# Gated DeltaNet heads in a fused trunk layer: alternating row groups, decays from running sums, no zero-state products

## The chip, the cores and the metric

The kernel runs on one core of a Trainium2 chip. The metric is the device time of one execution in microseconds (us). The profile is of one execution on the same core. The engines are called PE (TensorE), PEld (its weight loads), DVE (VectorE), ACT (ScalarE), POOL (GpSimd) and SP (SyncE, which issues all DMAs here).

## The reference

One layer over 2048 positions of width 1024: RMSNorm, one input projection, three mixers (differential attention, gated DeltaNet, RG-LRU), gates, an output projection with a residual, and a final RMSNorm. The change is in the gated DeltaNet, 4 heads of width 128, cut here to what matters. The reference works in chunks of 64 positions, the kernel in chunks of 128, which gives the same result.

```python
beta = jax.nn.sigmoid(b)
g = -jnp.exp(a_log) * jax.nn.softplus(a + dt_bias)
# in chunks:
g = jnp.cumsum(g, axis=-1)
decay = jnp.exp(jnp.where(tri, g[..., :, None] - g[..., None, :], -jnp.inf))
Lmat = jnp.where(strict, einsum('bhnid,bhnjd->bhnij', k_beta, k) * decay, 0.0)
T = triangular_solve(eye + Lmat, eye, lower=True, unit_diagonal=True)
u = T @ v_beta
w = T @ (k_beta * jnp.exp(g)[..., None])
a_intra = jnp.where(tri, einsum('bhnid,bhnjd->bhnij', q, k) * decay, 0.0)
def step(state, xs):                       # state starts at zero
    v_new = u_i - w_i @ state
    o = (q_i * jnp.exp(g_i)[..., None]) @ state + a_i @ v_new
    state = state * jnp.exp(g_last) + (k_i * jnp.exp(g_last - g_i)).T @ v_new
```

## The kernel before

The sequence is worked in two halves of 1024 positions, each half in two sub-blocks (`sb`) of 512, and these in chunks of 128, eight to a half (`NC_H`). The first stage, up to about 1165 us, is the projection with the DeltaNet and the LRU; the second is the attention with the output projection.

In the first stage a list of jobs, 40 to a half, is worked through in a written order. A job is one weight block; `unit` multiplies it with one sub-block of the normalized input: 24 fp32r matmuls of 128x512 (L298 to L300; every operand is split in a high and a low part). `unit` calls `pump` three times, and the loop over the jobs once after it. `pump` takes every background generator in `bgs` one step further, to its next `yield`; so `wait(4)` is about one unit. Jobs of DeltaNet heads (key, query, value, gate) stand between jobs of attention and LRU. With a head's first key unit `Gdn.start` puts its `main` on the list.

`gb_post` turns the columns b and a of a half into beta, the log decays `g` of all four heads, and by matmul with a triangle of ones (`tri_le`) their running sums in each chunk; `gam` is the exponential of these, `gl` that of the chunk's total. `ghi` and `glo` are g split in two.

`main` waits until the key and query sub-blocks of its head are projected, convolved (POOL's first tap in L359, DVE's three in L363), passed through a SiLU (L371, L375) and transposed for their norms by `key_t` (L449): `v.nt` is then 4. After that, for each sub-block, POOL multiplies `tri_le` by columns of `ghi` and of `glo` (L522, 8 products of 128x128), PE sums them with two fp32r matmuls against `tri_gt` (L528, L531), ACT takes the exponential (L535), and the result `dec` is the decay between any two positions of a chunk. The products of keys with keys and queries (L543) are multiplied by it (L549).

The inverse of the unit triangular matrices is made by blocks: 32x32 blocks by substitution on DVE (L590, L596), which are loaded into `pi` and transposed into `xi` (L613); then pairs of 32x32 blocks are joined to 64x64 by small fp32 matmuls (L626, a copy to `zs32`, L635), and these to 128x128 (L650, L658). The two pairs of a chunk lie on partitions 0 to 63 and 64 to 127; their matmuls contract over partitions 0 to 31 and 64 to 95 in L626, and over 32 to 63 and 96 to 127 in L635. All of the first pair's stand ahead of all of the second's. L639 makes the transposed joint block of the first pair once more by itself for `xi` (L643). Last, the chunks are walked in order with the state `st`: keys times state (L674), the solved values (L683), queries times state (L685), the state's new term (L692), the intra-chunk output (L693).

Tiles come from rings by tag and number of buffers (`tp`: 3 PSUM banks; `s16`: 16; `sd`: 1). Each engine's order is laid down by the framework when the kernel is built, by its own planned times of operands and buffers, not simply in the order of the text; only what is marked `keep_in_program_order` stays. Each engine then runs its instructions in that order and waits at the head of it. Other lines that the rows name: L117 fetches a weight block, L287 and L291 split it, L852 and L854 split the output weights, L775 to L777 are gates of the LRU, L317 to L319 the value projection.

## Time and profile before

| | |
|---|---|
| median of 3 runs | 1781.47 us (1778.9 to 1782.03) |
| the profiled execution | 1784.56 us |
| its span | 1782.8 us |
| mean granted clock of PE | 0.991 |
| PE, DVE, ACT, POOL busy | 97%, 73%, 55%, 20% |
| DMA, share of 16 engines | 49.5% |
| DMA moved | 257.45 MB |

Busy time is the time in which an engine has an instruction in work. Matmuls are pipelined, so that their times overlap: what one of them costs is the distance from its start to the next one's start. Durations and waits below are those of the profiled execution; its own time is its span and what lies around it.

### The profile page before, as it was taken

To read this page: it belongs to the slowest core of one execution; us is meant where nothing else is said; L and a number is where in the kernel's file an instruction comes from. 1 tells how busy PE (TensorE), PEld (TensorE's weight loads), DVE (VectorE), ACT (ScalarE), POOL (GpSimd) and SP (SyncE) were. 2 spreads that over 40 slices of the span, in tenths; PEclk is the share of its full clock that TensorE was granted. 3 is DMA by queue.
4 is the path that set the end of the run, shared out by engine and by line. 5 is a ranking of instruction groups with operands and counts; after the bars stand their busy time and mean duration, and the time that the engine had idled before them with its cause. 6 is when DMAs were issued, how large, how long until landed. Compare 5 with 4: busy or idle time off the path is not lost. (4 is left out here: it accounts for less than half of the span.)

```text
span 1782.8 us, 28375 instructions
## 1 busy us (share of the span) xinstructions
PE 1727.3 (97%) x9674; PEld 1440.2 (81%) x9674; DVE 1305.5 (73%) x3064; ACT 987.1 (55%) x2500; POOL 364.0 (20%) x591
## 2 busy tenths in 40 slices
PE   7999999999999899999999999989999999999998
PEld 6877778888888887887888888877888888887786
DVE  5576786776786656778687678658787877778896
ACT  6524524524535453452443443458878878878684
POOL 3222521400400212031040040011212213221011
PEclk9998999999999999999999999999999999999999
DMA  6146465133135432313313324597798797596442
GB/s 185 48 125 198 142 198 160 48 101 94 57 108 164 143 86 69 92 48 100 92 50 113 90 68 128 162 260 217 188 251 221 253 252 208 166 274 217 158 142 101
DMA packets 306901, 257.45 MB, mean 144 GB/s; under 512 B 66794, under 2 KB 242116, under 8 KB 306756
## 3 DMA queue, kind: packets, MB, share of 16 engines
q1 hardware_dynamic: 306756, 255.64, 49.5%
q8 instruction: 76, 1.25, 0.3%
q14 instruction: 69, 0.57, 0.1%
HBM read 171.69 MB, written 83.89 MB: 143 GB/s over the span
## 5 line engine op out<-in xcount | busy, mean ns | idle before, releaser
L298 PE MATMUL pj<-hp,wx 128*128 128x512 f32 x1120 | 465.6, 416 | 5.0 <-DVE s L375 2.9
L300 PE MATMUL pj<-hp,wx 128*128 128x512 f32 x1120 | 445.8, 398 | 0.0
L299 PE MATMUL pj<-hp,wx 128*128 128x512 f32 x1120 | 444.5, 397 | 0.0
L300 PEld LDWEIGHTS pj<-hp,wx 128*128 128x128 f32 x1120 | 211.4, 189 | 49.6
L298 PEld LDWEIGHTS pj<-hp,wx 128*128 128x128 f32 x1120 | 212.3, 190 | 48.3 <-DVE s L375 3.5
L299 PEld LDWEIGHTS pj<-hp,wx 128*128 128x128 f32 x1120 | 212.7, 190 | 41.6
L1030 DVE TENSOR_REDUCE nm<-s 128x1 f32<-128x512 f32 (+3 forms) x320 | 191.6, 604 | 27.5 <-PE s L1027 24.1
L1038 ACT ACTIVATE s<-s,nm 128x512 f32<-128x512 f32 (+3 forms) x272 | 170.6, 629 | 51.9 <-DVE nm L1030 50.7
L363 DVE SCALAR_TENSOR_TENSOR s<-raw,pcol,s 128x512 f32<-128x512 f32 x192 | 144.6, 753 | 36.3 <-POOL s L359 34.4
L1026 PE MATMUL s<-hp 128*128 128x512 f32 (+3 forms) x320 | 125.2, 392 | 6.2 <-ACT s L1038 3.1
L291 DVE TENSOR_TENSOR wx<-wx 128x1024 fp32r<-128x1024 f32 (+1 forms) x77 | 95.9, 1246 | 45.9 <-ACT wx L287 45.1
L287 ACT ACTIVATE wx<-wx 128x1024 fp32r<-128x1024 f32 (+1 forms) x76 | 80.5, 1059 | 80.5 <-PE pj L299 72.5
L1027 PE MATMUL s<-hp 128*128 128x512 f32 (+3 forms) x320 | 118.4, 370 | 0.0
L1101 PE MATMUL pt<-ident,s 128*128 128x128 f32 x544 | 86.4, 275 | 4.0 <-DVE s L1089 3.9
L354 POOL COPY halo<-raw 128x3 f32<-128x3 f32 x48 | 13.5, 281 | 374.0 <-ACT raw L352 364.9
L883 PE MATMUL pj<-g,wx 128*128 128x512 f32 x208 | 85.4, 411 | 0.0
L590 DVE TENSOR_TENSOR tt<-lt,tt 128x248 f32<-128x248 f32 (+30 forms) x248 | 80.4, 324 | 6.6
L596 DVE TENSOR_TENSOR tt<-tt 128x248 f32<-128x248 f32 (+30 forms) x248 | 79.2, 320 | 6.3
L1089 DVE SCALAR_TENSOR_TENSOR s<-s,cf,s 128x512 f32<-128x512 f32 (+2 forms) x112 | 75.1, 702 | 11.1 <-ACT s L1077 6.5
L885 PE MATMUL pj<-g,wx 128*128 128x512 f32 x208 | 82.3, 396 | 0.0
L884 PE MATMUL pj<-g,wx 128*128 128x512 f32 x208 | 82.0, 394 | 0.0
L317 PE MATMUL pj<-wx,hp 128*128 128x264 f32 (+1 forms) x256 | 77.1, 302 | 3.2 <-ACT hp L267 1.5
(341 smaller groups left out, 3966.5 us busy)
## 6 DMA issues: line engine op xcount, KB each, us to landing
wx<-in_w_in_dram SPq DMA_DIRECT2D x78, 512.0 KB, 4.1
wx<-y_sp SPq DMA_DIRECT2D x64, 512.0 KB, 5.5
hp<-k_sp SPq DMA_DIRECT2D x64, 256.0 KB, 6.3
wo_sp<-s SPq DMA_DIRECT2D x48, 256.0 KB, 2.5
v_sp<-s SPq DMA_DIRECT2D x64, 128.0 KB, 2.9
q_sp<-s SPq DMA_DIRECT2D x32, 256.0 KB, 3.6
k_sp<-s SPq DMA_DIRECT2D x32, 256.0 KB, 4.1
y_sp<-go SPq DMA_DIRECT2D x32, 256.0 KB, 2.1
```

The costliest lines, as they stand in the source:

```text
L291: pin(eng.tensor_tensor(wl, wr, wh.bitcast(F32), op=ALU.subtract))
L298: nc.tensor.matmul(ps, wh[:, kt, :], hb[kt][:, 0, :], start=(kt == 0), stop=False)
L299: nc.tensor.matmul(ps, wh[:, kt, :], hb[kt][:, 1, :], start=False, stop=False)
L300: nc.tensor.matmul(ps, wl[:, kt, :], hb[kt][:, 0, :], start=False, stop=(kt == KT - 1))
L363: nc.vector.scalar_tensor_tensor(y, raw[:, t : t + SB], pc(wcol(t)), y, op0=ALU.mult, op1=ALU.add)
L883: nc.tensor.matmul(ps, yh, wh, start=first, stop=False)
L885: nc.tensor.matmul(ps, yl, wh, start=False, stop=last)
L1026: nc.tensor.matmul(ps[:, :n], qq, kh[:, :n], start=True, stop=False)
L1027: nc.tensor.matmul(ps[:, :n], qq, kl[:, :n], start=False, stop=True)
L1030: nc.vector.tensor_reduce(nm[:, u, m, kb : kb + 1], ps[:, :n], axis=AX.X, op=ALU.max, negate=True)
L1038: nc.scalar.activation(ee[:, :n], ps[:, :n], AF.Exp, bias=nm[:, u, m, kb : kb + 1], accum_out=zp[:, u, m, kb : kb + 1],)
L1101: nc.tensor.transpose(pt[:, off + (u - us[0]) * P : off + (u - us[0] + 1) * P], e[(u, kt // 4)][:, (kt % 4) * P : (kt % 4 + 1) * P], ident,)
```

## The change

- The loops of L626 and L635 are turned round: chunk outside, pair inside, so that matmuls of the two row groups alternate in PE's order. A chunk's fp32 matmul is two instructions, so the alternation is by twos.
- L639 is dropped: the block for `xi` is a DVE transpose of the block that `pi` now holds.
- The decays no longer come from matmuls. `gb_post` makes one more matmul per half, the running sums of all heads and chunks as rows, copies them to SBUF and stores them in DRAM (`cs`). With a head's first key unit, two DMAs load the head's four rows for each sub-block, broadcast to all 128 partitions, into two buffers of `sd`. After `wait(4)` POOL subtracts in place each position's own sum (`cum`) and takes the minimum with zero (4 instructions of 128x128 for each sub-block, where 8 were), and ACT takes the exponential. `ghi`, `glo`, `tri_gt` and the `wait(3)` in front of the matmuls go.
- The first chunk of half 0 leaves out the two products with the zero state (L674, L685), and the last chunk of half 1 the state that nobody reads (L692, with its DVE operations). The four memsets of the state go.

```diff
--- before.py
+++ after.py
@@ -148,12 +148,6 @@
     nc.gpsimd.affine_select(
         tri_le, ones32, pattern=[[1, P]], compare_op=ALU.is_ge, fill=0.0, base=0, channel_multiplier=-1
     )
-    tri_gt = ctile([P, P], "tri_gt", F32R)
-    tri_gt32 = at([P, P], "s16", 16)
-    nc.gpsimd.affine_select(
-        tri_gt32, ones32, pattern=[[-1, P]], compare_op=ALU.is_gt, fill=0.0, base=0, channel_multiplier=1
-    )
-    nc.vector.tensor_copy(tri_gt, tri_gt32)
 
     pcol = ctile([P, N_COLS], "pcol")
     nps = psum.tile([P, SB], F32, name="pps", tag="tp", bufs=3)
@@ -172,8 +166,6 @@
     hlast = ctile([P, 4], "hlast")
     st2 = [at([P, 2, P], "st", 2) for _ in range(2)]
     st = [st2[h // 2][:, h % 2, :] for h in range(4)]
-    for h in range(4):
-        nc.gpsimd.memset(st[h], 0.0)
 
 
     def tp():
@@ -401,10 +393,6 @@
         g = at([P, 4, NC_H], "g", 2)
         nc.vector.scalar_tensor_tensor(g, xa, 0.0, ax, op0=ALU.max, op1=ALU.add)
         nc.vector.tensor_tensor(g, g, nea.unsqueeze(2).to_broadcast([P, 4, NC_H]), op=ALU.mult)
-        ghi = at([P, 4, NC_H], "ghi", 2, F32R)
-        nc.vector.tensor_copy(ghi, g)
-        glo = at([P, 4, NC_H], "glo", 2, F32R)
-        nc.vector.tensor_tensor(glo, g, ghi.bitcast(F32), op=ALU.subtract)
         yield
         yield
         yield
@@ -412,13 +400,21 @@
         gf = g.rearrange("p a b -> p (a b)")
         nc.tensor.matmul(pg[:, 0:32], tri_le, gf, start=True, stop=True)
         nc.tensor.matmul(pg[:, 32:64], ones, gf, start=True, stop=True)
+        nc.tensor.matmul(pg[0:32, 64 : 64 + P], gf, tri_le, start=True, stop=True)
         gam = at([P, 2, 4, NC_H], "gam", 2)
         nc.scalar.activation(
             gam, pg[:, 0:64].rearrange("p (a b c) -> p a b c", a=2, b=4), AF.Exp
         )
+
+        cum = at([P, 4, NC_H], "cum", 1)
+        nc.scalar.activation(cum, pg[:, 0:32].rearrange("p (b c) -> p b c", b=4), AF.Copy)
+        cr = at([32, P], "s16", 16)
+        nc.scalar.activation(cr, pg[0:32, 64 : 64 + P], AF.Copy)
+        cs = dram.tile([4 * NC_H, P], F32, name="cs", tag="cs", bufs=2)
+        nc.sync.dma_start(cs, cr)
         ngam = at([P, 4, NC_H], "ngam", 2)
         nc.vector.tensor_scalar_mul(ngam, gam[:, 0], -1.0)
-        r.beta, r.ghi, r.glo, r.gam, r.gl, r.ngam = beta, ghi, glo, gam[:, 0], gam[:, 1], ngam
+        r.beta, r.cum, r.cs, r.gam, r.gl, r.ngam = beta, cum, cs, gam[:, 0], gam[:, 1], ngam
         r.ready = True
 
 
@@ -488,7 +484,26 @@
 
         def main(v):
             h, gbs = v.h, v.gbs
-            while v.nt < 4 or not gbs.ready:
+            while not gbs.ready:
+                yield
+            decs = [at([P, 4, P], "sd", 2) for _ in range(2)]
+            for sb in range(2):
+                r0 = h * NC_H + sb * 4
+                nc.sync.dma_start(
+                    decs[sb].rearrange("p c e -> p (c e)"),
+                    gbs.cs[r0 : r0 + 4].rearrange("r e -> (r e)").unsqueeze(0).to_broadcast([P, SB]),
+                )
+            yield from wait(4)
+            for sb in range(2):
+                for c in range(4):
+                    ci = sb * 4 + c
+                    nc.gpsimd.tensor_scalar(
+                        decs[sb][:, c, :], decs[sb][:, c, :], gbs.cum[:, h, ci : ci + 1], 0.0,
+                        op0=ALU.subtract, op1=ALU.min,
+                    )
+                nc.scalar.activation(decs[sb], decs[sb], AF.Exp)
+                yield
+            while v.nt < 4:
                 yield
             ss = v.ss
             nc.vector.tensor_scalar_add(ss, ss, 4e-6)
@@ -514,25 +529,8 @@
                 kq = v.kq[sb]
                 la = at([P, 4, 2, P], "g5", 5)
                 las.append(la)
-                gmh = at([P, 4, P], "s16", 16, F32R)
-                gml = at([P, 4, P], "s16", 16, F32R)
-                for c in range(4):
-                    ci = sb * 4 + c
-                    for gm, gg in ((gmh, gbs.ghi), (gml, gbs.glo)):
-                        nc.gpsimd.tensor_scalar(
-                            gm[:, c, :], tri_le, gg.bitcast(F32)[:, h, ci : ci + 1], 0.0,
-                            op0=ALU.mult, op1=ALU.add,
-                        )
-                yield from wait(3)
-                pe = tp()
-                nc.tensor.matmul(
-                    pe, tri_gt, gmh.rearrange("p c e -> p (c e)"), start=True, stop=False
-                )
-                nc.tensor.matmul(
-                    pe, tri_gt, gml.rearrange("p c e -> p (c e)"), start=False, stop=True
-                )
-                dec = at([P, 4, P], "sd", 1)
-                nc.scalar.activation(dec, pe.rearrange("p (c e) -> p c e", c=4), AF.Exp)
+
+                dec = decs[sb]
                 nc.vector.tensor_tensor(
                     cd[:, sb * 4 : sb * 4 + 4], cc[:, sb * 4 : sb * 4 + 4], dec[:, :, P - 1],
                     op=ALU.mult,
@@ -621,8 +619,8 @@
             ]
             zs32 = at([P, NC_H, 32], "zs", 1)
             pz = tp().rearrange("p (c e) -> p c e", c=NC_H)
-            for a, b in pairs:
-                for c in range(NC_H):
+            for c in range(NC_H):
+                for a, b in pairs:
                     nc.tensor.matmul(
                         pz[b, c, 0:32], lt_ab(c, a, b), xi[a, c, a], start=True, stop=True
                     )
@@ -630,19 +628,15 @@
                 nc.vector.tensor_copy(zs32[b], pz[b, :, 0:32])
             yield
             pu = tp().rearrange("p (c e) -> p c e", c=NC_H)
-            for a, b in pairs:
-                for c in range(NC_H):
+            for c in range(NC_H):
+                for a, b in pairs:
                     nc.tensor.matmul(
                         pu[a, c, 0:32], zs32[b, c, :], pi[b, c, b], start=True, stop=True
                     )
-            for c in range(NC_H):
-                nc.tensor.matmul(
-                    pu[32:64, c, 0:32], pi[32:64, c, 32:64], zs32[32:64, c, :],
-                    start=True, stop=True,
-                )
-            nc.vector.tensor_scalar_mul(xi[32:64, :, 0:32], pu[32:64, :, 0:32], -1.0)
             for a, b in pairs:
                 nc.vector.tensor_scalar_mul(pi[a, :, b], pu[a, :, 0:32], -1.0)
+
+            nc.vector.transpose(xi[32:64, :, 0:32], pi[0:32, :, 32:64])
             yield
             lo, up = slice(0, 64), slice(64, 128)
             pz = tp().rearrange("p (c e) -> p c e", c=NC_H)
@@ -670,36 +664,51 @@
                 so = at([P, 4], "so", 2)
                 for c in range(4):
                     ci = sb * 4 + c
-                    pks = psum.tile([P, P], F32, name="ch", tag="ch", bufs=2)
-                    nc.tensor.matmul(pks, v.kq[sb][:, c, 0, :], S_, start=True, stop=True)
+
+                    none, final = v.hf == 0 and ci == 0, v.hf == 1 and ci == NC_H - 1
                     ct = at([P, 4, P], "ct", 2)
-                    br = ct[:, 0, :]
-                    nc.vector.scalar_tensor_tensor(
-                        br, pks, gbs.ngam[:, h, ci : ci + 1], v.vb[sb][:, c, :],
-                        op0=ALU.mult, op1=ALU.add,
-                    )
-                    yield
+                    br = v.vb[sb][:, c, :]
+                    if not none:
+                        pks = psum.tile([P, P], F32, name="ch", tag="ch", bufs=2)
+                        nc.tensor.matmul(pks, v.kq[sb][:, c, 0, :], S_, start=True, stop=True)
+                        br = ct[:, 0, :]
+                        nc.vector.scalar_tensor_tensor(
+                            br, pks, gbs.ngam[:, h, ci : ci + 1], v.vb[sb][:, c, :],
+                            op0=ALU.mult, op1=ALU.add,
+                        )
+                        yield
                     py = psum.tile([P, P], F32, name="ch", tag="ch", bufs=2)
                     nc.tensor.matmul(py, pi[:, ci, :], br, start=True, stop=True)
                     po = psum.tile([P, 2, P], F32, name="oq", tag="oq", bufs=1)
-                    nc.tensor.matmul(po[:, 0, :], v.kq[sb][:, c, 1, :], S_, start=True, stop=True)
-                    yd = ct[:, 1, :]
-                    nc.vector.tensor_scalar(yd, py, cd[:, ci : ci + 1], None, op0=ALU.mult)
+                    if not none:
+                        nc.tensor.matmul(
+                            po[:, 0, :], v.kq[sb][:, c, 1, :], S_, start=True, stop=True
+                        )
+                    if not final:
+                        yd = ct[:, 1, :]
+                        nc.vector.tensor_scalar(yd, py, cd[:, ci : ci + 1], None, op0=ALU.mult)
                     y = ct[:, 2, :]
                     nc.scalar.activation(y, py, AF.Copy)
                     yield
-                    pst = psum.tile([P, P], F32, name="ch", tag="ch", bufs=2)
-                    nc.tensor.matmul(pst, v.kp[sb][:, c, :], yd, start=True, stop=True)
+                    if not final:
+                        pst = psum.tile([P, P], F32, name="ch", tag="ch", bufs=2)
+                        nc.tensor.matmul(pst, v.kp[sb][:, c, :], yd, start=True, stop=True)
                     nc.tensor.matmul(po[:, 1, :], las[sb][:, c, 1, :], y, start=True, stop=True)
-                    nc.vector.scalar_tensor_tensor(
-                        S_, S_, gbs.gl[:, h, ci : ci + 1], pst, op0=ALU.mult, op1=ALU.add
-                    )
-                    ay = ct[:, 3, :]
-                    nc.scalar.activation(ay, po[:, 1, :], AF.Copy)
-                    nc.vector.scalar_tensor_tensor(
-                        os_[:, c, :], po[:, 0, :], gbs.gam[:, h, ci : ci + 1], ay,
-                        op0=ALU.mult, op1=ALU.add,
-                    )
+                    if none:
+                        nc.vector.tensor_copy(S_, pst)
+                    elif not final:
+                        nc.vector.scalar_tensor_tensor(
+                            S_, S_, gbs.gl[:, h, ci : ci + 1], pst, op0=ALU.mult, op1=ALU.add
+                        )
+                    if none:
+                        nc.scalar.activation(os_[:, c, :], po[:, 1, :], AF.Copy)
+                    else:
+                        ay = ct[:, 3, :]
+                        nc.scalar.activation(ay, po[:, 1, :], AF.Copy)
+                        nc.vector.scalar_tensor_tensor(
+                            os_[:, c, :], po[:, 0, :], gbs.gam[:, h, ci : ci + 1], ay,
+                            op0=ALU.mult, op1=ALU.add,
+                        )
                     jk = at([P, SB], "junk", 1, BF16)
                     nc.scalar.activation(
                         jk[:, :P], os_[:, c, :], AF.Square, accum_out=so[:, c : c + 1]
@@ -913,7 +922,7 @@
                     if last:
                         nw.append(load_wo(4 + e, 1, e) if dh == 0 else load_wo(e % 4, e // 4, e))
                     yield
-                pe = at([P, SB], "sd", 1)
+                pe = at([P, SB], "sd", 2)
                 nc.scalar.activation(pe, ps, AF.Copy)
                 nc.gpsimd.tensor_tensor(xx, pe, xx, op=ALU.add)
                 late.append(partial(nc.sync.dma_start, xo_sp[rows, cols], xx))
```

## Rows read from the trace of the kernel before

**Rows 1.** Page, part 1: busy us, share of the span, instructions of each engine.
```profile
PE 1727.3 (97%) x9674; PEld 1440.2 (81%) x9674; DVE 1305.5 (73%) x3064; ACT 987.1 (55%) x2500; POOL 364.0 (20%) x591
```

**Rows 2.** Windows by stage: stretch, us, busy us (instructions) by engine, PEclk, DMA.
```profile
60.00:230.00 170.00, 163.88 (x835) 131.29 (x834) 119.17 (x268) 75.93 (x187) 59.27 (x97) 0.97 0.44 135
...
820.00:1165.00 345.00, 344.50 (x1957) 284.55 (x1956) 251.10 (x600) 141.44 (x328) 52.75 (x104) 1.00 0.35 102
```

**Rows 3.** Waits of PE: line <- who released it: us, times, longest.
```profile
PE tp L635 <- POOL s L854: 2.1, 1, 2.1
...
PE tp L528 <- POOL s L522: 1.4, 3, 0.6
...
PE tp L543 <- DVE g L549: 0.9, 4, 0.2
```

**Rows 4.** Timeline of PE in the second head's inverse: start us, us, instruction.
```profile
284.87 1.09 PE L626 MATMUL tp<-xi,g 32*32 32x32 f32 x32
...
288.88 1.00 PE L635 MATMUL tp<-g,zs 32*32 32x32 f32 x29
289.69 0.21 PE L639 MATMUL tp<-zs,g 32*32 32x32 f32 x1
289.72 0.19 PE L635 MATMUL tp<-g,zs 32*32 32x32 f32 x1
...
289.81 0.57 PE L639 MATMUL tp<-zs,g 32*32 32x32 f32 x13
```

**Rows 5.** Timeline of PE at a decay product.
```profile
355.02 0.40 PE L528 MATMUL tp<-s,tri_gt 128*128 128x512 f32 x1
355.26 0.39 PE L531 MATMUL tp<-s,tri_gt 128*128 128x512 f32 x1
355.87 1.97 PE L543 MATMUL tp<-g 128*128 128x256 f32 x8 [0.22 <-DVE g L549]
```

**Rows 6.** Timeline of PE at a state product.
```profile
177.60 0.38 PE L674 MATMUL ch<-st,g 128*128 128x128 f32 x2
177.74 0.48 PE L298 MATMUL pj<-hp,wx 128*128 128x512 f32 x1
178.05 0.40 PE L299 MATMUL pj<-hp,wx 128*128 128x512 f32 x1
178.29 0.40 PE L300 MATMUL pj<-hp,wx 128*128 128x512 f32 x1
```

**Rows 7.** Groups by line: busy us, mean ns of one, idle before.
```profile
L522 POOL TENSOR_SCALAR s<-tri_le,glo 128x128 fp32r<-128x128 f32 x64 | 31.5, 492 | 0.0
L522 POOL TENSOR_SCALAR s<-tri_le,ghi 128x128 fp32r<-128x128 f32 x64 | 27.2, 426 | 0.4 <-issue 0.4
...
L613 DVE STREAM_TRANSPOSE xi<-g 32x256 f32<-32x256 f32 x24 | 10.4, 434 | 10.5 <-DMA g<-ts 10.0
```

**Rows 8.** DMA issues: KB each, median us to landing.
```profile
hp<-k_sp SPq DMA_DIRECT2D x64, 256.0 KB, 6.3
...
s<-in_w_out_dram SPq DMA_DIRECT2D x24, 256.0 KB, 3.6
```

**Rows 9.** Waits of SP's queue: us, times, longest.
```profile
SPq L117 <- DVE wx L291: 184.5, 32, 17.0
```

**Rows 10.** Timeline of a key sub-block of the first head.
```profile
77.78 0.69 DVE L375 SCALAR_TENSOR_TENSOR g<-s,s 128x512 f32<-128x512 f32 x1 [0.70 <-ACT s L371]
...
80.39 0.60 PE L449 MATMUL tp<-ident,g 128*128 128x128 f32 x4
```

**Rows 11.** Windows in the first head, behind the stall of L635.
```profile
161.50:170.50 9.00, 9.00 (x43) 6.81 (x42) 3.45 (x6) 0.60 (x1) 1.23 (x4) 0.50 0.82 193
```

**Rows 12.** Timeline of PE in that stretch.
```profile
162.08 0.63 PE L299 MATMUL pj<-hp,wx 128*128 128x512 f32 x1
162.50 0.63 PE L300 MATMUL pj<-hp,wx 128*128 128x512 f32 x1
```

**Rows 13.** Groups by line: the split of the output weights.
```profile
L852 ACT ACTIVATE s<-s 128x512 fp32r<-128x512 f32 x24 | 14.9, 622 | 6.2 <-DMA s<-in_w_out_dram 6.2
```

## The prediction, before the change was run

> **What bounds the kernel now.** I read the busy shares first. TensorE is busy for 97% of the span, DVE for 73%, ACT for 55% and POOL for 20% [rows 1]. A busy TensorE need not be a full one, so the table by stage comes next: in the last projection stretch it is busy for 344.5 of 345 us at full granted clock, and in the stretch with the first head for 163.9 of 170 us at 0.97 [rows 2]. There a unit of 24 fp32r matmuls follows the next, start to start 0.23 to 0.24 us [rows 6], which is the time the 512 columns take; the 0.40 us that the rows give as duration is a pipeline and not a cost. So in the first 1165 us, where every edited line runs, TensorE issues almost without a hole, and an instruction removed from its queue is worth its start-to-start distance. The waits of TensorE on the edited lines are short [rows 3]. DVE, ACT and POOL matter only where one of them is late for a TensorE instruction. I expect nothing in the attention stage, where the edits only give `sd` a second buffer.
>
> **Sum, part by part.** The profiled execution took 1784.56 us (span 1782.8, 1.8 around it), 0.17% above the median 1781.47 of the runs shown. I sum against the profiled time and then take the same off the median.
>
> *Alternating row groups and the dropped block.* An fp32 matmul is two instructions here. L626 is 2 pairs x 8 chunks x 2 = 32 of them per head. From first start to last start they take 1.09 - 0.19 = 0.90 us (the last end less the 0.19 us that one lasts, as the single rows show). L635 and L639 are 48 and take from 288.88 to 290.38 - 0.19, which is 1.31 us [rows 4]. Within one row group the step is (0.57 - 0.19)/12 = 0.032 us, from the thirteen L639. But where the last L635 (partitions 96 to 127) meet the first L639 (32 to 63), the two mix: L639 at 289.69, an L635 at 289.72 that lasts 0.19 as ever, and so on. Two row groups thus run beside each other, and what hinders that today is only the order: the second group's instructions stand 16 places behind, and begin when three of the first are left. In the new order pairs of instructions alternate, so the two groups should overlap throughout: 16 x 0.032 = 0.51 us plus a little for the later group, 0.53. Per head that saves 0.90 - 0.53 = 0.37 and 1.31 - 0.53 = 0.78 us (L639 gone with it), together 1.15, and 8 heads (4 heads x 2 halves) give **9.2 us**. The bounds are no overlap at all (32 x 0.032 = 1.02 us a block, so 1.31 + 0.90 - 2.04 = 0.17 a head, **1.4 us**) and a perfect one (0.48 a block, 1.25 a head, 10.0 us). I take a value near the upper end because the overlap is in the rows. The DVE transpose that now fills the block of `xi` costs 0.43 us [rows 7], where a scaling of the same 32x256 elements stood; it comes after the two scalings of `pi` rather than before them, about 0.9 us later (two more DVE operations of that size), while a yield puts six matmuls or 1.4 us in front of the next block.
>
> The Trainium skill, TensorEngine Tiling (Array Packing), section Restrictions and Gotchas, speaks against this part: different row tiles, it says, cannot access the same PSUM bank at the same time. Both pairs write one bank of `pz` or `pu`. By that rule the lower bound 1.4 us would hold in place of 9.2. The trace disagrees so far: the mixed L635 and L639 of rows 4 write one `pu` tile. The skill's TensorE: Matmul & The Clock Gate, Part 1 (on the gap of 56 ns), adds that start-to-start never falls under about 25 ns; an estimate from that page is 0.8 us a block and some 5 us of gain. The mixed rows, 0.01 to 0.03 apart, are under it for a few instructions only.
>
> *Decays.* L528 and L531 go: 16 pairs (8 heads x 2 sub-blocks), 0.24 us each [rows 5], so 32 x 0.235 = 7.5 us. Their waits go too: 1.4 us for POOL's products, and 0.9 us that L543 stood for a PSUM buffer of which L531's tile held one of three [rows 3]. Together **9.8 us**, with 7.5 as lower bound if those waits find another owner. POOL's 128 products at 0.43 to 0.49 us [rows 7] become 64 subtract-and-min of the same shape: some 29 us less on an engine at 20%. The Exp stays on ACT, reading SBUF. Sixteen broadcast loads of 256 KB are new on SP's queue, and two 16 KB stores; they add 4.2 MB. What that can cost is the third rival.
>
> *Zero state.* For the first chunk of each head in half 0, two fp32 matmuls go (4 heads x 2), and for the last chunk in half 1 one (4 heads): 12. One costs 0.22 us: L674 starts at 177.60 and L299 at 178.05, 0.45 us with one L298 of 0.23 in between [rows 6]. **2.6 us.** DVE work removed here is off the path.
>
> *Added.* The transposed running sum is one fp32 matmul per half, 2 x 0.22 = **0.4 us** lost. The copies of `cum` and `cr` are small ACT work in front of it.
>
> Sum: 9.2 + 9.8 + 2.6 - 0.4 = 21.2 us. 1784.56 - 21.2 = 1763.4 for a profiled execution; 1781.47 - 21.2 = 1760.3 for the median, and I say **1760.5**.
>
> **What could be late next.** Each engine runs an order that the framework lays down while building, from its own planned times, so edits can move neighbours. One bad spot of before shows the size: in the first head L635 stood 2.1 us, by the row for POOL's L854 [rows 3], and behind that the granted clock is 0.50 from 161.5 to 170.5 us [rows 11], which of the two levels is 1.2 GHz; the wide matmuls there start 0.42 us apart [rows 12] in place of 0.23. Nine us at that pace hold the work of 4.9, so 4.1 us were lost, with the stall 6.2. If this spot goes, that much comes back; if another like it arises, as much is lost. I take zero and keep both ends, 1754 and 1767.
>
> **Rivals.** (a) *The row groups do not overlap*, by bank or by issue: 21.2 - (9.2 - 1.4) = 13.4 us, so **1768**. Against it stand the mixed rows; for it, that they show only a few instructions. Chance 0.10, with a partial overlap, between 1761 and 1768, included. Both pages' rules above end in this rival.
> (b) *The neighbourhood is laid out better*: the stall and the half clock of the first head vanish, **1754**. The second head's L635, at 288.88 [rows 4], has no wait in its row. Chance 0.10.
> (c) *The broadcast comes late and holds POOL* (the other side). The new subtractions wait in POOL's order for a 256 KB load issued four yields earlier, 4 x 6 matmuls, 5.6 us. Such loads land in 3.6 to 6.3 us after issue [rows 8], and SP's own queue can stand up to 17 us before a weight load [rows 9]. Behind POOL's waiting instruction stand the key convolution's first tap (L359), then DVE's taps, the SiLU and TensorE's transposes of the key (L449). The slack is small: the SiLU result for one sub-block ended at 78.47 and its transposes began at 80.39, 1.9 us [rows 10]. A load that is d us late on POOL costs TensorE d - 1.9. With 16 of them, d = 1.9 + 21.2/16 = 3.2 us eats the whole gain, and 4 us each gives 1760.3 + 16 x 2.1 = **1794**. Against it: the 24 loads of output weights, also 256 KB and used six yields after issue, let ACT wait 6.2 us in all [rows 13]; four yields is only 2.8 us less, and the planner can put the tap first. Chance 0.07.
> (d) *Removed work turns into waits*: TensorE reaches the DVE results of the inverse sooner and stands there, so that nine tenths of the 21.2 us are given back, **1779** (no change). DVE has 27% free [rows 1], which speaks against it. Chance 0.05.
> The forecast itself has 0.68.
>
> **Range and chances.** 0.2% of 1781, 3.6 us, is about what a measurement of this kernel can tell from no change. The range takes in (a) and (b) and some late broadcasts (half the case (c), one us beyond the slack each, 1776): 1752 to 1775. Faster: forecast, (a), (b) 0.88. Same: 0.05. Slower: 0.07.
>
> **What would show it.** Right: 32 instructions per inverse block within 0.75 us (0.53 plus the tail), and no third block; TensorE with 180 instructions fewer (32 + 128 + 24 - 4); the new POOL subtractions without idle time for a DMA before them; the last projection stretch again full, and the attention stage as long as before. Wrong: blocks still 0.9 us or longer (a); POOL idle before the subtractions for the broadcast and L449 waiting for DVE (c); new waits of TensorE on DVE in the inverse (d). The prediction fails most easily by a stall with a clock fall behind it, in either direction, since one is a third of the whole gain.

## The result, and the profile after

The changed kernel takes 1795.04 us (median of 4 runs, 1793.55 to 1795.3) beside 1781.75 us for the kernel before (4 runs, 1778.9 to 1785.72): **1.0053 times as long, 95% interval 1.0037 to 1.0069**. The forecast was 1760.5 us, range 1752 to 1775, with 0.07 for slower: wrong in sign. The profiled execution took 1795.14 us, its span 1793.3 us at a mean granted clock of 0.989.

The work went as forecast. Part 1 of the page after has the 180 TensorE instructions fewer that were counted [rows 1]:

```profile
PE 1712.6 (96%) x9494; PEld 1421.5 (79%) x9494; DVE 1298.1 (72%) x3043; ACT 987.3 (55%) x2504; POOL 350.9 (20%) x522
```

The blocks of the inverse overlap. TensorE's timeline in the second head (the lines L624 and L633 are L626 and L635 of [rows 4]) shows one block of 32 in 0.69 - 0.19 = 0.50 us where 0.53 was said, and no third block:

```profile
275.08 0.69 PE L624 MATMUL tp<-xi,g 32*32 32x32 f32 x32
...
279.12 0.69 PE L633 MATMUL tp<-g,zs 32*32 32x32 f32 x32 [0.37 <-issue]
```

Eleven of the sixteen blocks take this time. The other five take 0.75 to 1.34 us, with projection matmuls or waits of 0.2 to 0.5 us between their first instructions and the rest.

The table by stage (columns as in [rows 2]) shows what did not go as forecast: the last projection stretch has holes. TensorE is busy for 347.8 of 355 us, where before 344.5 of 345, and in the stretch with the first head for 159.5 of 170, where before 163.9:

```profile
60.00:230.00 170.00, 159.53 (x811) 127.27 (x809) 117.98 (x266) 75.70 (x188) 54.01 (x85) 0.98 0.46 139
820.00:1175.00 355.00, 347.83 (x1934) 284.46 (x1934) 256.57 (x618) 146.93 (x339) 47.75 (x87) 1.00 0.36 104
```

The waits of TensorE after name the largest. In the changed kernel the projection of [rows 6] stands at L290 to L292, the value projection at L309, the key products at L541 and their scaling at L547; the wait of L541 is the 0.9 us of L543 in [rows 3], grown to 13.8:

```profile
PE tp L541 <- DVE g L547: 13.8, 7, 5.0
...
PE pj L309 <- DVE s L325: 4.7, 2, 3.4
...
PE tp L445 <- DVE g L367: 2.6, 2, 2.4
```

To see all holes at once I took from the records, for each line of TensorE, the median distance from one start to the next. The median times the count, summed over the lines, is "work"; what a distance has above its line's median, where that is over 0.3 us, is a stall. Beside them stands the time at the granted clock 0.50, the lower of the two levels (1.2 GHz); some 2 us of it lie behind the last instruction in every run.

| kernel | span | work | stalls | at clock 0.50 |
|---|---|---|---|---|
| before | 1782.8 | 1696.2 | 51.4 | 33.9 |
| after | 1793.3 | 1677.8 | 80.3 | 41.6 |

Work fell by 18.4 us; the prediction's removed and added instructions come to 21.2 - 2.3 of waits = 18.9. Stalls rose by 28.9 us, and 7.7 us more at half the clock cost about half of that, 3.9. The three come to +14.4; the span rose by 10.5, and I put the remaining -3.9 down to small distances and double counts. So the loss is stalls, and nearly all of it, 28.2 of the 28.9 us, arises in the first stage. Set beside each other in their order, the wide projection matmuls of after start 6 us later at about 103 us of the kernel before, 3.5 us later at 566 us near the end of half 0, 13.4 us later at 684 us in the first head of half 1, and 12.6 us later at the end of that stage; the last matmuls of the attention stage start 10.0 us later.

The timeline of the engines at the first head of half 0 shows the longest of the new stalls:

```profile
77.28 5.78 POOL L500 TENSOR_SCALAR sd<-sd,cum 128x128 f32<-128x128 f32 x8 [2.08 <-DMA sd<-cs]
...
80.78 0.60 PE L445 MATMUL tp<-ident,g 128*128 128x128 f32 x4
...
83.09 0.63 ACT L504 ACTIVATE sd<-sd 128x512 f32<-128x512 f32 x1 [2.12 <-POOL sd L500]
...
84.11 0.27 ACT L448 ACTIVATE junk<-tp 128x128 bf16<-128x128 f32 x1
...
85.76 1.09 PE L541 MATMUL tp<-g 128*128 128x256 f32 x4
...
87.40 0.17 DVE L509 TENSOR_SCALAR gss<-gss 128x16 f32<-128x16 f32 x1
...
87.61 1.02 DVE L92 TENSOR_SCALAR rn<-gss 128x16 int32<-128x16 int32 x1
...
87.64 0.95 POOL L582 MEMSET g<- 128x1024 f32 x1
88.66 0.17 DVE L96 TENSOR_TENSOR nw_t<-rn 128x16 f32<-128x16 f32 x1
...
89.18 0.69 DVE L367 SCALAR_TENSOR_TENSOR s<-s,s 128x512 f32<-128x512 f32 x1
...
91.28 0.16 DVE L514 TENSOR_TENSOR cc<-cc,beta 128x8 f32<-128x8 f32 x1
...
91.56 1.65 DVE L547 SCALAR_TENSOR_TENSOR g<-tp,cc,sd 128x256 f32<-128x256 f32 x4
...
92.57 2.05 PE L541 MATMUL tp<-g 128*128 128x256 f32 x4 [5.02 <-DVE g L547]
```

Read it from the end. At 92.57 L541 has stood 5.02 us for DVE's L547. L541 writes keys times keys and queries into tiles of `tp`, of which there are three; L547 is what reads a tile and sets it free. L547 cannot start before the norms of the head are through, a chain of small DVE operations from L509 (87.40) to L514 (91.28): three rounds of L96 to L98, 0.17 us each, with L92 in front and other work (L367) between them. L92 took 1.02 us there, beside POOL's memset L582. The kernel before had `wait(3)`, some 18 wide matmuls, in front of each sub-block's products. There the same chain ran with these matmuls beside it. The edit took the sums of the decays and that wait together; the products then start 1.3 us behind the last transposes (L445), where the kernel before has 6.5. Its norm chain was through, with L499, before its products began:

```profile
81.08 0.28 ACT L452 ACTIVATE junk<-tp 128x128 bf16<-128x128 f32 x1 [1.24 <-PE tp L449]
...
86.99 0.15 DVE L499 TENSOR_TENSOR cc<-cc,beta 128x8 f32<-128x8 f32 x1
...
87.44 1.89 PE L543 MATMUL tp<-g 128*128 128x256 f32 x8
```

In this head the chain also came late. ACT's squares of the last transposed sub-block (L448, before L452), of which the norms are sums, began 2.7 us behind the end of the transposes, where before they began 0.1 us behind it. ACT's Exp L504 stood ahead of them for POOL's subtractions L500, which took 5.78 us after a wait of 2.08 us for their load. So the products came 4.8 us earlier than before (82.64 and 87.44), and the chain ended 4.3 us later (91.44 and 87.14). In the other seven heads, which have 8.8 of the 13.8 us, the squares begin at most 0.5 us behind the transposes. The 5.02 us of standing are followed by the lower clock, and DVE is denser there. The table of windows, in columns as before, shows the 6.8 us behind that stall at 0.50, and ten microseconds behind the first products of the last head:

```profile
91.50:98.30 6.80, 5.73 (x14) 4.53 (x15) 4.67 (x11) 1.54 (x2) 2.39 (x4) 0.50 0.13 19
...
1055.00:1065.00 10.00, 8.21 (x39) 6.67 (x38) 9.10 (x31) 2.82 (x6) 2.73 (x5) 1.00 0.06 10
```

The same ten microseconds of the kernel before (L543 in the place of L541), where TensorE is busy for 9.75 in place of 8.21 us:

```profile
1050.00:1060.00 10.00, 9.75 (x46) 7.88 (x45) 8.54 (x22) 2.99 (x8) 8.63 (x15) 1.00 0.23 60
```

**The broadcast loads** were the prediction's rival (c). POOL does wait for them, and ACT for POOL, as the list of waits over all engines shows:

```profile
ACT sd L504 <- POOL sd L500: 36.8, 13, 6.4
...
POOL sd L500 <- DMA sd<-cs: 31.8, 9, 8.1
```

TensorE pays for it in two places: in the late chain of the first head above, and at the first head of half 1. This timeline shows the second: L500 holds ACT's Exp L504 (2.13), behind which L344 and with it the key's path stand, and TensorE's L445 waits 2.41 us:

```profile
663.72 5.03 POOL L500 TENSOR_SCALAR sd<-sd,cum 128x128 f32<-128x128 f32 x7
...
668.78 0.63 ACT L504 ACTIVATE sd<-sd 128x512 f32<-128x512 f32 x1 [2.13 <-POOL sd L500]
...
669.32 0.58 ACT L344 ACTIVATE raw<-pj 128x512 f32<-128x512 f32 x1
...
673.94 0.69 DVE L367 SCALAR_TENSOR_TENSOR g<-s,s 128x512 f32<-128x512 f32 x1 [0.69 <-ACT s L363]
...
674.78 0.71 PE L445 MATMUL tp<-ident,g 128*128 128x128 f32 x4 [2.41 <-DVE g L367]
```

That stall and the 3.4 us at half clock behind it are some 4 us of the 28.9 + 3.9. The new POOL operation is dearer than I priced it (mean 0.79 us, median 0.714, against 0.43 to 0.49 of [rows 7]; so POOL's work fell by 9 us, not 29), which the group's row shows:

```profile
L500 POOL TENSOR_SCALAR sd<-sd,cum 128x128 f32<-128x128 f32 x64 | 49.5, 790 | 31.8 <-DMA sd<-cs 31.8
```

### The profile page after: what moved, and what is told of

It reads as the page before. It is cut to its first block, busy times and chain, and to the rows that moved or that the text cites. A ratio compares the mean times of both kernels' runs of the same rounds, so it can differ in the third digit from the quotient of the medians.

```text
span 1793.3 us, 27951 instructions
## 1 busy us (share of the span) xinstructions
PE 1712.6 (96%) x9494; PEld 1421.5 (79%) x9494; DVE 1298.1 (72%) x3043; ACT 987.3 (55%) x2504; POOL 350.9 (20%) x522
## 4 chain that ended last, share of the span: by engine, by line
PE 59%; DVE 15%; issue 9%; ACT 7%; DMA 4%; POOL 4%; SPq 1%; POOLq 0%; DVEq 0%; ACTq 0%
PE pj L291 10%; PE pj L290 10%; PE pj L292 9%; PE pj L894 3%; PE pj L892 3%; PE pj L893 3%; DVE s L355 2%; PE s L1035 2%; PE s L1036 2%; PE pt L1110 2%; DVE tt L594 1%; DVE tt L588 1%; DMA wx<-xo_sp 1%; PE pj L309 1%; PE pj L311 1%
## 5 line engine op out<-in xcount | busy, mean ns | idle before, releaser
L290 PE MATMUL pj<-hp,wx 128*128 128x512 f32 x1120 | 465.3, 415 | 6.0 <-DVE sz L367 3.7
L292 PE MATMUL pj<-hp,wx 128*128 128x512 f32 x1120 | 446.7, 399 | 0.0
L290 PEld LDWEIGHTS pj<-hp,wx 128*128 128x128 f32 x1120 | 212.4, 190 | 49.1 <-DVE sz L367 4.6
L292 PEld LDWEIGHTS pj<-hp,wx 128*128 128x128 f32 x1120 | 211.7, 189 | 47.9
L309 PE MATMUL pj<-wx,hp 128*128 128x264 f32 (+1 forms) x256 | 78.2, 306 | 9.2 <-DVE s L325 4.7
```

The source lines that it names most:

```text
L290: nc.tensor.matmul(ps, wh[:, kt, :], hb[kt][:, 0, :], start=(kt == 0), stop=False)
L292: nc.tensor.matmul(ps, wl[:, kt, :], hb[kt][:, 0, :], start=False, stop=(kt == KT - 1))
```

## The experiments

Three theories stood against each other. A: the lost `wait(3)` was a cover for DVE's norm chain, and its loss is the loss. B: the broadcast loads hold POOL, ACT and the key. C: the order that the framework lays down for each engine comes out differently for any edit, and what it does to other lines outweighs the edit. Ratios are against the kernel before in runs on the same chip, with 95% intervals; stalls, work and half clock as above, of one profiled execution each, which lies up to 5.7 us (e18) from its run's median.

| run | ratio | interval | median us | work | stalls | at 0.50 |
|---|---|---|---|---|---|---|
| e1_cover_each | 0.9916 | 0.9898 to 0.9933 | 1770.72 | 1677.7 | 60.0 | 28.0 |
| e2_cover_first | 1.0026 | 1.0010 to 1.0042 | 1790.82 | 1675.0 | 73.6 | 37.6 |
| e3_no_decay_edit | 1.0011 | 1.0001 to 1.0021 | 1786.82 | 1687.4 | 62.3 | 26.1 |
| e4_decay_alone | 1.0109 | 1.0096 to 1.0123 | 1805.77 | 1686.8 | 81.6 | 44.0 |
| e5_groups_alone | 0.9943 | 0.9922 to 0.9963 | 1776.57 | 1687.4 | 53.7 | 30.5 |
| e6_cover_old_blocks | 0.9971 | 0.9954 to 0.9987 | 1780.25 | 1683.2 | 59.2 | 30.0 |
| e7_short_chain | 1.0007 | 0.9994 to 1.0020 | 1786.52 | 1679.4 | 73.2 | 47.7 |
| e8_cover_one | 1.0067 | 1.0048 to 1.0086 | 1798.11 | 1676.3 | 79.8 | 38.2 |
| e9_zero_alone | 1.0054 | 1.0037 to 1.0072 | 1795.50 | 1694.5 | 62.6 | 37.3 |
| e10_keep_yield | 0.9972 | 0.9959 to 0.9985 | 1780.17 | 1684.9 | 59.7 | 41.1 |
| e11_cover_no_zero | 0.9964 | 0.9949 to 0.9978 | 1779.73 | 1679.2 | 64.6 | 44.9 |
| e12_cover_two | 0.9996 | 0.9979 to 1.0013 | 1785.58 | 1676.8 | 74.1 | 40.0 |
| e13_cover_behind | 0.9988 | 0.9978 to 0.9999 | 1782.43 | 1673.7 | 69.7 | 37.0 |
| e14_cover_four | 1.0096 | 1.0079 to 1.0113 | 1801.39 | 1676.9 | 83.2 | 50.4 |
| e15_cover_keep_yield | 0.9950 | 0.9932 to 0.9967 | 1776.45 | 1676.9 | 61.3 | 43.4 |
| e16_before_two | 1.0231 | 1.0209 to 1.0252 | 1822.01 | 1698.3 | 87.8 | 29.7 |
| e17_before_four | 1.0032 | 1.0018 to 1.0047 | 1787.51 | 1693.9 | 55.4 | 21.1 |
| e18_before_no_yield | 1.0075 | 1.0059 to 1.0091 | 1794.47 | 1696.8 | 55.6 | 29.8 |

### Parts of the change, and the cover

**e1_cover_each**, the changed kernel with the wait put back:

```diff
                 las.append(la)
+                yield from wait(3)
                 dec = decs[sb]
```

> The changed kernel with wait(3) put back in front of each sub-block's key products, where the kernel before had it. Theory A (cover): those three yields, 18 matmuls, were what TensorE did while DVE finished the norm chain that the first scaling of the products needs; without them the third product waits for a PSUM buffer. Then the 13.8 us of waits at the products fall under 2, the half clock behind the first of them (6.8 us, 3.4 lost) goes, and the time is about 1795 - 17 = 1778 (1774 to 1783). Theory B (late broadcasts hold POOL and with it the key convolution): no change, 1790 to 1797. Theory C (the order was re-laid for the worse in many places): the waits at the products go, but others take their place, 1785 or more.

Measured 0.9916: faster than both kernels, and than A's range. TensorE's waits show the products' 13.8 us gone (0.3 left):

```profile
PE tp L541 <- DVE g L547: 0.3, 1, 0.3
```

In the ten microseconds behind the last head's first products TensorE is full again, with DVE busier than before (windows, as above):

```profile
1037.00:1047.00 10.00, 10.00 (x48) 8.36 (x47) 9.45 (x22) 2.15 (x6) 2.84 (x4) 1.00 0.24 59
```

A is supported for the place of the stall, though the 24 us between the two kernels (1.0053 and 0.9916) are more than the 13.8 of that row. Against the kernel before, 0.84% of 1784.94 us is a gain of 15 us where the sum said 21.2.

**e2_cover_first**, the same wait, in front of the first sub-block only (`if sb == 0:`).

> wait(3) in front of the first sub-block's products alone. A: the chain is made once per head, so one cover is enough; within 3 us of the kernel with the wait in both sub-blocks, 1775 to 1783. B: 1790 to 1797. C: 1785 or more.

Measured 1.0026, and the wait stays. In this kernel's waits the products are L542:

```profile
PE tp L542 <- DVE g L548: 9.0, 6, 3.7
```

Two tiles, the first sub-block's, find room; it is the second sub-block's products that must not come before the chain is through, and one cover at the start does not do it. The expectation was wrong there.

**e3_no_decay_edit**, the kernel before with the blocks and the zero state, the decays still by matmul.

> The kernel before with the alternating row groups, the dropped block and the products with the zero state left out, but the decays still by matmul. A: both edits give what they take from TensorE, 9.6 and 2.6 us: 1769 to 1773. B: the same. C: half of it or less is seen, 1776 or more.

Measured 1.0011. 8.8 us of work are gone and nothing is gained. TensorE's waits name POOL's products for the decays (L520 here, L522 before; L526 is L528):

```profile
PE tp L526 <- POOL s L520: 10.0, 6, 2.3
```

POOL's timeline in the third head of half 1 shows why. The mask L555 stands ahead of seven of the eight L520 of the second sub-block, and POOL is idle for 5.14 us before it:

```profile
919.95 0.37 POOL L520 TENSOR_SCALAR s<-tri_le,ghi 128x128 fp32r<-128x128 f32 x1
...
925.46 0.97 POOL L555 TENSOR_SCALAR_AFFINE_SELECT g<-g 128x512 f32<-128x512 f32 x1 [5.14 <-PE pj L298]
...
926.42 0.37 POOL L520 TENSOR_SCALAR s<-tri_le,glo 128x128 fp32r<-128x128 f32 x1
...
928.58 0.50 PE L526 MATMUL tp<-s,tri_gt 128*128 128x512 f32 x1 [2.28 <-POOL s L520]
```

In the kernel before the eight (L522) stand ahead of the mask (L557), and L528 has no wait:

```profile
926.09 0.37 POOL L522 TENSOR_SCALAR s<-tri_le,ghi 128x128 fp32r<-128x128 f32 x1
...
929.82 0.37 POOL L522 TENSOR_SCALAR s<-tri_le,glo 128x128 fp32r<-128x128 f32 x1
...
930.39 0.40 PE L528 MATMUL tp<-s,tri_gt 128*128 128x512 f32 x1
...
931.25 0.63 POOL L557 TENSOR_SCALAR_AFFINE_SELECT g<-g 128x512 f32<-128x512 f32 x1 [1.06 <-PE tp L531]
```

The mask stands between the products at all six places where L526 waits, with waits of 0.7 to 2.3 us; in the kernel before it does so at two, for 0.6 us each. Nothing in the edit names these lines. This is theory C, with its place.

**e4_decay_alone**, the kernel before with the decay edit alone.

> The kernel before with the new decays alone. A: saves 9.8 - 0.4, loses 13.8 of waits at the products and 3.4 by the clock: 1782 + 8 = 1790 (1786 to 1795). B: also slower, but with waits of the key transposes and not of the products. C: anywhere within 8 us of 1782.

Measured 1.0109, the dearest of the three parts, and 1805.8 us, above what A and C expected. The products' wait (L543 here) is there again, with a second long one at the projection, for DVE's SiLU:

```profile
PE tp L543 <- DVE g L549: 15.3, 7, 5.0
PE pj L292 <- DVE sz L369: 8.3, 2, 7.4
```

### The size of the blocks, the chain and the cover

**e5_groups_alone**, the kernel before with the blocks alone.

> The kernel before with the alternating row groups and the dropped block alone: the decays stay products on TensorE with their wait(3), the zero state is multiplied. If removed TensorE work is worth its start-to-start distance (the prediction), the blocks' 9.2 us come off the kernel before, about 1775 us (0.995). If what decides is where the framework lays POOL's products in its re-laid order (theory C; the earlier run without the decay edit stood 10.0 us for them and gained nothing), the gain is again eaten: 1782 to 1787, with a row of TensorE waiting for POOL's s L520 of several us. The blocks themselves should show 32 instructions in about 0.5 us either way.

Measured 0.9943, 10 us of 1784.56 (interval 7 to 14), with 8.8 us less work and stalls almost as before (53.7). The prediction's 9.2 us are right: here, with stalls as before, the removed work was worth its distance.

**e6_cover_old_blocks**, e1_cover_each with the old blocks and L639.

> The changed kernel with wait(3) before each sub-block's products, but with the old order of the inverse's blocks and the third block back. Against the run with the cover and the new blocks (1770.7 us) the prediction's block term says 9.2 us more, about 1780. If the gain there hung on the cover alone and the blocks are free because TensorE waits elsewhere, it stays at 1771. TensorE's blocks should take 0.9 and 1.3 us again. No row of TensorE at the key products waiting for g should come back (under 2 us) if the cover is what removes it.

Measured 0.9971, 9.5 us more than with the new blocks (the intervals allow 5 to 14). The block term holds a second time.

**e7_short_chain**, the changed kernel with a shorter chain (the call alone is shown; the helper takes the number of steps, one in place of three):

```diff
-            rsqrt(A, rn, ss, "gn")
+            rsqrt(A, rn, ss, "gn", 1)
```

> The changed kernel with no cover, but with one Newton step in place of three in the inverse root of the query and key norms; this leaves part of the computation out (q and k are normalised less precisely), so its time alone is read. It takes six DVE operations of 0.17 to 0.2 us, about 1.1 us, out of the chain that stands between the products of a head and the DVE operation that reads them. Theory A (the key products stand for a buffer of PSUM until that chain is through): the row of the key products waiting for g falls from 13.8 us in 7 waits by about 1.1 us each, to 5 to 7 us, and the time by 7 to 10 us, 1785 to 1788. Theory C (the re-laid order, not the chain): the row and the time stay, 1793 to 1797.

Measured 1.0007, 8.2 us less than the changed kernel (1.0053 - 1.0007 of 1784.56), and the wait halved as A says:

```profile
PE tp L541 <- DVE g L547: 6.7, 4, 4.5
```

**e8_cover_one**, the changed kernel with one `yield` where e1 has `wait(3)`.

> The changed kernel with one yield (one unit of TensorE work, six wide matmuls, about 1.4 us) before each sub-block's products, where the kernel before had wait(3). Theory A: a third of the cover takes up to 1.4 us from each of the head's waits, of which the median is 1.9; the row of the key products waiting for g falls from 13.8 to about 4 to 6 us, and the time to about 1783, between 1795 without cover and 1771 with three. If the waits only move from the first to the second sub-block, as with the cover in front of the first alone, it stays near 1791.

Measured 1.0067: no gain. The products' wait fell to 3.2 us, as said, but the next user of `tp`, a transpose, stands for the same L547, and the rest went to other lines (stalls 79.8 in place of 80.3):

```profile
PE tp L469 <- DVE g L547: 4.5, 4, 1.2
...
PE tp L541 <- DVE g L547: 3.2, 3, 2.2
```

A is right on where the first stall is and wrong on what removing it gives.

### Zero state, and more of the cover

**e9_zero_alone**, the kernel before with the zero-state edit alone.

> The kernel before with the zero-state edit alone (first chunk of half 0 without its two products and its yield, last chunk of half 1 without the state that nobody reads). By the prediction's price 12 products of 0.22 us go: 2.6 us less, ratio 0.9985. Theory C: the two earlier runs on the kernel before differ by this edit alone (blocks alone 0.9943, blocks and zero state 1.0011), so it costs some 12 us there by re-laying the order; alone it should then give about 1.006, with a row of TensorE waiting for POOL's products of the decays (s L522) of several us where the kernel before has 2.1.

Measured 1.0054 with 9.8 us in 6 waits for POOL's products, as C said. This edit, priced at a gain of 2.6, costs 9.6 us.

**e10_keep_yield**, e3_no_decay_edit with the first chunk's `yield` kept:

```diff
                         )
-                        yield
+                    yield
                     py = psum.tile([P, P], F32, name="ch", tag="ch", bufs=2)
```

> The run without the decay edit (blocks and zero state, 1.0011), with the yield kept that the zero-state edit drops in the first chunk. Theory C in its narrow form: it is the missing yield that moves the first head's chain by one step and with it POOL's order; with the yield back the time is that of the blocks alone less 2.6 us, about 0.9925, and the wait for POOL's products s (10.0 us in 6 waits) is under 2 us. If the removed products or memsets themselves move the order, the time stays near 1.001 and the waits stay.

Measured 0.9972, nearly halfway from 1.0011 to the 0.9925 expected. The two long waits of half 0 (at 352 and 482 us in e3) are gone, those of half 1 stay:

```profile
PE tp L526 <- POOL s L520: 5.9, 4, 2.3
```

**e11_cover_no_zero**, e1_cover_each without the zero-state edit.

> The changed kernel with wait(3) before each sub-block's products, without the zero-state edit: blocks and decays with cover. If the edit is worth its products, 2.6 us more than with it, about 0.993. If it costs here what it costs on the kernel before (some 12 us), about 0.985. If its cost comes by POOL's products for the decays, which this kernel does not have, the first: 0.993.

Measured 0.9964. With the cover the zero-state edit gives 0.5%, 8.6 us, more than its products; without it costs. Neither expectation named this.

**e12_cover_two**, e1_cover_each with `wait(2)`.

> The changed kernel with wait(2) before each sub-block's products. Without cover it takes 1.0053 of the kernel before, with one yield 1.0067, with three 0.9916. Theory A, with the chain's length as the threshold (the longest waits of the first head 5 us, the others 1.2 to 2.1, so two yields of 1.4 us cover all but the longest): 0.993 to 0.998, and under 3 us of TensorE waiting for g. Theory C (the number of yields matters by the order that is laid out, not by the time it covers): near 1.005, with waits of TensorE at other lines.

Measured 0.9996, between. 2.3 us of the products' wait are left, as A says, but the time is above A's range: stalls are 74.1, most at other lines.

### Place, number, and the order itself

**e13_cover_behind**, the changed kernel with the six yields behind the products:

```diff
             nc.gpsimd.memset(pi, 0.0)
-            yield from wait(4)
+            yield from wait(10)
```

> The changed kernel with the six yields that its two lost wait(3) were, put behind the key products (wait(10) in place of wait(4) before the substitution). The steps of a head are as many as with the cover, but nothing stands before the products. If the place counts (theory A: work of TensorE must lie between the projections of a head's queries and its products, while DVE runs the norm chain), the wait of the products for g stays at 10 to 14 us and the time at 1793 to 1798. If only the number of steps counts, by spreading DVE's work of a head over more of TensorE's, it comes to 1771 to 1778 as with wait(3) in front.

Measured 0.9988. The wait at the products stays, so its cover is a matter of place:

```profile
PE tp L541 <- DVE g L547: 11.4, 6, 5.0
```

The time fell by 0.65% all the same, to 1782.4 us, between the two ranges. So the number of steps counts too, by what it does elsewhere.

**e14_cover_four**, e1_cover_each with `wait(4)`.

> The changed kernel with wait(4) before each sub-block's products: the next step after 1.0053, 1.0067, 0.9996 and 0.9916 for none, one, two and three yields. If three yields cover the chain (no wait of the products for g was left there), a fourth gives nothing: 0.990 to 0.994. If the time goes with the number of yields through the order that is laid out, it moves by more than 0.4% either way.

Measured 1.0096. The wait at the products is gone altogether, and the kernel is the slowest of those with a cover. Its largest wait is at the projection, for the SiLU:

```profile
PE pj L290 <- DVE s L367: 11.3, 4, 5.5
```

**e15_cover_keep_yield**, e1_cover_each with the first chunk's `yield` kept, as in e10.

> The changed kernel with wait(3) before each sub-block's products, and with the yield kept that the zero-state edit drops in the first chunk of half 0. On the kernel before the missing yield cost some 7 us (1.0011 with blocks and no yield, 0.9972 with it). If that came by POOL's products for the decays, which do not exist here, the yield changes nothing: 0.990 to 0.994. If a head's step by itself moves the order, it goes towards the run without the zero-state edit (0.9964).

Measured 0.9950, between 0.9916 and 0.9964, with its interval touching that of each: not decided.

**e16_before_two**, no work added or removed:

```diff
-                yield from wait(3)
+                yield from wait(2)
                 pe = tp()
```

> The kernel before with wait(2) in place of wait(3) before the sums of the decays, everything else as it was: no TensorE work is added or removed. If a wait's yields matter only as cover, one yield of 1.4 us less per sub-block lets at most the waits at L528 and L543 grow by a few us: 1.000 to 1.004. If the order that is re-laid decides, the time may move by up to 1% either way, with new waits of TensorE at lines that this edit does not touch.

Measured 1.0231, the largest difference of all, 41 us, outside both expectations. Work is the same (1698.3), stalls rose by 36. The waits say POOL:

```profile
PE tp L528 <- POOL s L522: 21.4, 12, 2.7
```

and POOL's timeline in the third head of half 1 shows the pattern of e3: one product, then the mask L557, which waits 3.65 us, then the other seven, and L528 behind them:

```profile
949.45 0.37 POOL L522 TENSOR_SCALAR s<-tri_le,ghi 128x128 fp32r<-128x128 f32 x1
...
953.46 0.96 POOL L557 TENSOR_SCALAR_AFFINE_SELECT g<-g 128x512 f32<-128x512 f32 x1 [3.65 <-DVE g L549]
...
954.41 0.37 POOL L522 TENSOR_SCALAR s<-tri_le,glo 128x128 fp32r<-128x128 f32 x1
...
956.59 0.79 PE L528 MATMUL tp<-s,tri_gt 128*128 128x512 f32 x1 [2.51 <-POOL s L522]
```

The mask stands there at six of the twelve waits, with 13.0 of the 21.4 us. The other six, 1.3 to 1.6 us each, have no mask: there the first sub-block's L528 simply reaches POOL's products too soon. In e17, with four yields, the mask stands there nowhere and L528 never waits for POOL. That the planned times of the framework let the mask overtake is my reading; they were not seen.

**e17_before_four**, the same line with `wait(4)`.

> The kernel before with wait(4) in place of wait(3): no work is added or removed. As cover it can only help: 0.998 to 1.000. If the order decides, up to 1% either way; the changed kernel with four yields instead of three lost 1.8%.

Measured 1.0032, above A's range: more cover, and slower.

**e18_before_no_yield**, the kernel before without the `yield` of the first chunk of half 0, all products kept.

> The kernel before without the yield of the first chunk of each head in half 0, with all of its products: the step that the zero-state edit drops, alone. The zero-state edit alone gave 1.0054, and the yield put back into blocks and zero state took 0.4% off. If the missing yield is most of that edit's loss, about 1.004 with 5 to 10 us of TensorE waiting for POOL's products s; if the removed products or memsets do it, 0.999 to 1.001.

Measured 1.0075, more than the 1.004 expected, with 5.4 us of waits for POOL's products (the profiled execution was its shortest, so the stalls in the table are low). In the kernel before, the dropped yield accounts for the loss of the zero-state edit: 1.0054 is 1.0075 less 0.2%, and that edit's 12 products were priced at 0.15%. With the new blocks it accounts for a part only: e10, with the yield kept and 12 products fewer, is still 0.3% slower than e5 (the intervals overlap by 0.04%).

## Why the prediction was wrong

**The step that failed.** The sum took every removed TensorE instruction at its distance and let the order stand. Two removals were not instructions, and the sum gave them no price: the `wait(3)` before the products, and the `yield` of the first chunk. The prediction said in the decays that "Their waits go too" (1.4 and 0.9 us), but never asked what the wait itself had covered. The first cost 13.8 us of waits at the products (shown: gone with the cover back in e1, smaller with the shorter chain in e7, nearly unchanged, 11.4 us, with the yields behind in e13), and putting it back gave 24 us. That cover alone does not make the kernel fast: in e14 the wait is gone too, and the time is 1.0096. The second costs 0.75% alone in the kernel before (e18). In the changed kernel with cover, keeping it made nothing faster (e15), so it is not shown to be a part of this loss.

**The other half of the failure is a size.** Under "What could be late next" the prediction said that the order is laid down anew and "I take zero and keep both ends, 1754 and 1767", that is, 6.2 us. The runs show that spread to be several times wider: with the same TensorE work, none to four yields before the products give 1.0053, 1.0067, 0.9996, 0.9916 and 1.0096, and one yield fewer in the kernel before gives 1.0231. Three yields are the best of the values tried in both kernels. By these runs, a range for an edit of this kernel that moves a step is at least ±1%.

**Point by point.**
- *The stage is bound by TensorE, and removed work is worth its distance.* Right as far as it goes: work fell by 18.4 us for 18.9 forecast.
- *Blocks, 9.2 us.* Right: 10 us in e5, 9.5 between the medians of e6 and e1; a block takes 0.50 us for 0.53. Rival (a) is out. In a block, instructions start 7 and 25 ns apart in turn (L624) or 3 and 29 (L633), 16 ns in the mean, and both row groups write one bank of PSUM, in different partitions. That speaks against the rule on row tiles and one bank in the Trainium skill (TensorEngine Tiling (Array Packing), Restrictions and Gotchas), at least as a matter of time. The floor of 25 ns (the Trainium skill, TensorE: Matmul & The Clock Gate, Part 1) does not hold for every second start here, at 3 to 7 ns; the step within one row group, 32 ns in the kernel before, is above it.
- *Decays, 9.8 us.* The work is no less than said: e4 has 9.4 us less than before, where 7.5 - 0.4 was forecast. The time is wrong by sign: +1.09% alone. With the cover, three pairs of runs differ by the decays alone, and they do not agree: +0.2% without the zero-state edit (e11 and e5), -0.2% with it and its yield kept (e15 and e10), -0.95% with it whole (e1 and e3). In the first two the intervals overlap; the third is the one clear gain, 17 us. What decides was not settled; e11 has 11 us more of stalls than e5, and its largest rows, 6.7 and 5.0 us, are the projection's for DVE's SiLU.
- *Zero state, 2.6 us.* The work is 1.7 us less in e9 and no less between e5 and e3. The edit costs 0.5 to 0.7% with the old decays (e9; e3 against e5) and gains 0.5% with the new ones and the cover (e1 against e11).
- *Rival (b), the neighbourhood.* It came in part: the stall of L635 in the first head and the half clock behind it are gone in the changed kernel. But others arose, and the time at half clock in the first stage rose from 17.0 to 23.8 us.
- *Rival (c), the broadcast.* The wait exists (31.8 us on POOL, 36.8 on ACT), and mostly TensorE did not feel it; it paid about 4 us at the first head of half 1, and a part of the 5.02 us in the first head, where the chain ended 4.3 us late by POOL's subtractions and their load. B is not the whole cause, since e1 keeps all loads and gains; what it adds without the cover was not tried by itself.
- *Rival (d), work turns into waits.* The nearest to what happened, but for another reason and too small: not DVE's inverse, but its norm chain and the re-laid order.
- *What would show it.* The count (180) and the attention stage came true, and the block length in eleven of sixteen. The subtractions "without idle time for a DMA before them" did not, nor did "the last projection stretch again full", which was the right thing to look at. The range's end, 1775, also left out the 1776 that the text names for late broadcasts.

What stays open: which single planned time makes an order good or bad. The runs show two patterns (the mask in front of POOL's products; the products in front of the norm chain) and their prices, but not the whole of the scatter in e8, e12, e14 and e15.

## What to carry to other kernels

A wait or a yield that an edit removes is an edit of its own: look at what ran under it, and who next holds the buffers behind it, before summing what became shorter. Where a framework lays out each engine's order from planned times, first move one wait by one in the untouched kernel: here that alone gave +2.3% and +0.3%, and it sets how wide a forecast for any edit must be. And try the cover beside the edit: the same change with the wait put back was 0.8% faster than the kernel before, where without it it was 0.5% slower.

## What the runs showed of the hardware

- Matmul instructions on two row groups of TensorE that alternate by pairs start 16 ns apart in the mean (7 and 25 in turn in L624, 3 and 29 in L633), half the 32 ns within one group, with one PSUM bank as their target, in different partitions. So the two groups run beside each other.
- A small DVE operation can be held by one of POOL: in the timeline above L92, on 128x16, took 1.02 us, where the median of its eight is 0.176. POOL's memset L582 (0.95 us) began 0.03 us after it and ended 0.04 us before it. The same happens in the third head (344.72 us, 1.02 us). In four heads the memset began 0.09 to 0.16 us after L92, which took 0.17 to 0.18; in the kernel before and in e1, where the memset falls elsewhere, the eight take 0.17 to 0.19. The Trainium skill's page SBUF — State Buffer (SBUF: two separate sides) says that DVE's tensor-scalar operations in a two-port mode and POOL's block each other for a whole instruction. The trace agrees in the length; whether L92 ran in such a mode no record shows, and by the records L92 began first, so that by that page the memset should have been the one to wait.
- POOL's subtract-and-min on 128x128, in place, costs 0.71 us at least; its multiply-and-add out of a constant tile costs 0.37 in the timelines above. Why was not tried.
